# SSM stage with real and imaginary parts stacked on 128 partitions, in a two-block kernel on one core

## The chip, the cores and the metric

One NeuronCore of a Trainium2 chip runs the whole program, one launch for each call. The metric is the device time of that core in microseconds (us), from the kernel's runs on the chip. Engines are named as in the profile: PE is the matrix engine, PEld its weight loads, DVE, ACT and POOL are VectorE, ScalarE and GpSimd, and SP is the queue engine that starts most of the weight transfers.

## What is computed

The program runs two transformer-like blocks on 512 tokens (and 16 meta tokens in front) with a model width of 1024. The first block mixes a chunked gated linear attention (GLA, four heads) with a grouped diagonal state space layer (SSM), and then has a feed-forward part. The second block has latent attention, a causal convolution and a mixture of 32 experts. Only the SSM of the first block is touched here. Cut to what matters, the reference is:

```python
# 64 groups of 16 channels, 64 complex states for each group
lam = exp(dt * (a_re + 1j * a_im))                 # per group and state
bb  = (lam - 1) / (a_re + 1j * a_im) * (b_re + 1j * b_im)
x_t = lam * x_{t-1} + bb @ u_t                     # 64 states, complex
y_t = Re(c @ x_t) + d_skip * u_t
g_s = gelu(y)                                      # on to a gated linear unit
```

## The kernel before

Matrix products of the large weights are made from an upper and a lower part of each operand (three products, `mm3`, lines 93 to 100), in a stream of 128x128 weight loads with up to 512 columns. `Weights` (line 503) loads a block of 1 MB on SP's queue, ACT makes the upper part (line 74) and DVE the lower one (line 75), one block ahead of its use. Both rings have two buffers.

The SSM works on chunks of eight tokens. There are 64 groups; groups q and q + 32 make a pair, and eight *eighths* of four pairs go through the same steps:

- `sincos_exp` (line 144) makes the powers lambda^0..8 (`pw`) and the scaled B (`bb`), with the states of the two groups of a pair on partitions 0 to 63 and 64 to 127 and the real and the imaginary part in the free dimension. Lines 269 to 273 lay `bb` out as a block-diagonal operand `bd`, cleared by POOL and copied by ACT.
- `ssm_states` (line 277) makes the state that each chunk contributes, `ssm_scan` (line 323) carries it through the chunks on POOL: 64 dependent steps of three small operations each.
- `ssm_prep` (line 334) makes C times the powers, `CL`, by six operations on 128x576 elements (lines 350 to 356). They run on DVE; for the first two eighths (`EARLY`) five of the six run on POOL. Eight products of `CL` with `bd` (line 362), real part and then imaginary part summed, give a *strip* of taps, 32 rows (two groups of 16) by 128 for each pair. ACT copies the strip (line 366), DVE adds the skip weights (line 367), and POOL's queue stores it into `k_dram` (line 368).
- `ssm_load` (line 372) reads u from DRAM on POOL's queue, and from `k_dram` eight shifted copies of the strips as the Toeplitz matrices `Tb`, half of them on SP's queue and half on POOL's (line 379).
- `ssm_main` (line 384) has ACT copy the carried states into a block-diagonal operand `HB` (line 390). For each pair it makes two products of 64 weight columns with `Tb` (line 396), one in each column half of the array, and then two of 128 weight columns with `HB` against `CL` (line 400), real and imaginary. ACT applies the gelu and stores the rows.

All of these operands are full fp32: each such product is two instructions on PE, here called *passes*. `ssm_out` (line 411) strings prep, load and main together with two yields in each eighth, and `block` weaves it between steps of the large products: the projections and chains of the GLA heads, then `z_gla` and `mix_gla`, one step being 24 products of 512 columns in the last two. `HB` is one tile, cleared once by POOL on lines 2110 to 2112, behind the scan in POOL's program. The order of each engine's instructions is set when the program is built, by a scheduler that takes what is ready in the order of the text; `issue_after` pins a few places. Every engine then runs its list in order.

The lines that the steps below touch most:

```python
  M = nc.gpsimd if ei < EARLY else V
  ...
  nc.tensor.matmul(p[:32, q * 128:(q + 1) * 128], lhsT=e.bd[:, ri, q0 + q]..., rhs=CL[:, ri, q, 0:8]..., start=(ri == 0), stop=(ri == 1))
  ...
  nc.tensor.matmul(y[64 * g2:64 * g2 + 64, ...], lhsT=U[:, g2, q, 2:66], rhs=T[:, q, g2, :], ...)
  nc.tensor.matmul(o, lhsT=HB[:, q, ri, :], rhs=CL[:, ri, q, 1:9]..., ...)
```

Of the kernel before, what the change touches and what calls it, by code (L numbers as in the profile page):

```python
# [57 lines left out]
def helpers(e):  # L58
# [62 lines left out]
    def rsqrt_act(pool, sumsq, inv_n, n, p=128):  # L121
        """1 / sqrt from ScalarE's square root and one step of Newton's."""
# [21 lines left out]
def sincos_exp(e, sp, mid, keep):  # L144
    """lambda = exp(dt (a_re + i a_im)), bbar, and the powers lambda^0..8, on [128 (g2, n), 32 q]."""
# [123 lines left out]
    bd = keep.tile([128, 2, 32, 2, 16], F32, name="bd", bufs=1)  # L269
    nc.gpsimd.memset(bd, 0.0)  # L270
    for g2 in range(2):
        P = slice(64 * g2, 64 * g2 + 64)
        nc.scalar.copy(bd[P, :, :, g2], bb[P])
    e.pw, e.lam, e.bb, e.bd = pw, lam, bb, bd


def ssm_states(e, sp):
    """Chunk-end states: sum_j lambda^(7-j) bbar u_j, into e.H[:, c, ri, q]; an eighth of the pairs at a step."""
# [55 lines left out]
def ssm_prep(e, sp, ei):  # L334
    """The Toeplitz matrices (taps inside a chunk) and the carry-in matrices of the pairs of eighth ei."""
    nc, A = e.nc, e.A
    V = nc.vector
    q0 = 4 * ei
    cr = sp.tile([128, 2, 4, 16], F32, name="craw", bufs=2)
    nc.gpsimd.dma_start(cr, A["ssm_c"][:, :, q0:q0 + 4, :])  # L340
    dsk = sp.tile([32, 4, 16], F32, name="dsk", bufs=2)
    nc.gpsimd.dma_start(dsk, A["d_diag"][:, q0:q0 + 4, :])
    CL = sp.tile([128, 2, 4, 9, 16], F32, name="CL", bufs=2)
    t = sp.tile([128, 4, 9, 16], F32, name="CLt", bufs=1)
    pr = e.pw[:, 0, :, q0:q0 + 4].rearrange("p k q -> p q k")[:, :, :, None].to_broadcast([128, 4, 9, 16])
    pi = e.pw[:, 1, :, q0:q0 + 4].rearrange("p k q -> p q k")[:, :, :, None].to_broadcast([128, 4, 9, 16])
    c_r = cr[:, 0][:, :, None, :].to_broadcast([128, 4, 9, 16])
    c_i = cr[:, 1][:, :, None, :].to_broadcast([128, 4, 9, 16])
    M = nc.gpsimd if ei < EARLY else V
    M.tensor_mul(CL[:, 0], pr, c_r)  # L350
    M.tensor_mul(t, pi, c_i)
    M.tensor_sub(CL[:, 0], CL[:, 0], t)
    t2 = sp.tile([128, 4, 9, 16], F32, name="CLt", bufs=1)
    M.tensor_mul(CL[:, 1], pr, c_i)
    M.tensor_mul(t2, pi, c_r)
    V.scalar_tensor_tensor(CL[:, 1].rearrange("p q k h -> p (q k h)"),
                           CL[:, 1].rearrange("p q k h -> p (q k h)"), -1.0,
                           t2.rearrange("p q k h -> p (q k h)"), op0=OP.mult, op1=OP.subtract)
    p = e.ps()
    for q in range(4):  # L360
        for ri in range(2):
            nc.tensor.matmul(p[:32, q * 128:(q + 1) * 128],
                             lhsT=e.bd[:, ri, q0 + q].rearrange("p g h -> p (g h)"),
                             rhs=CL[:, ri, q, 0:8].rearrange("p k h -> p (k h)"), start=(ri == 0), stop=(ri == 1))
    stt = sp.tile([32, 4, 128], F32, name="strip", bufs=1)
    nc.scalar.copy(stt, p[:32].rearrange("p (q n) -> p q n", q=4))
    V.tensor_add(stt[:, :, 0:16], stt[:, :, 0:16], dsk)
    nc.gpsimd.dma_start(e.k_dram[q0:q0 + 4, :, 112:240].rearrange("q g n -> g q n"), stt)
    return CL

# [52 lines left out]
def row_rms(e, pool, parts, n, d_inv, rsqrt=None):  # L423
    """1 / sqrt(mean of squares + eps) of n rows given in parts along the free axis."""
# [10 lines left out]
def normed(e, pool, x, g_row, sh_row=None, rsqrt=None):  # L435
    """rmsnorm of 128 token rows x by g_row (plus sh_row)."""
# [10 lines left out]
def turn(e, xs, hi, lo, t):  # L447
    """Token tile t transposed and split into hi, lo[:, k, t * 128..]."""
# [15 lines left out]
def proj_f(e, w, m, xn, spans):  # L464
    """Columns m*128.. of the weight block w as features on partitions; one PSUM tile for each span of tokens."""
# [2063 lines left out]
```

## Time and profile before

| what | value |
|---|---|
| runs | 1563.92, 1561.77, 1563.57 us; median 1563.57 |
| span of the profiled execution | 1561.5 us (its own time is not listed apart from the three runs, which lie 0.3 to 2.4 us above the span) |
| PE busy | 1477.2 us, 95% of the span |
| DVE, ACT, POOL busy | 889.9, 647.6, 541.4 us |
| mean granted clock of PE | 0.977 |
| PE busy from 276.3 to 428.0 us | 151.68 of 151.70 us |

The span runs from the first instruction to the last. Busy time is the union of an engine's instructions; matmuls overlap in it, so a row's duration is longer than the step from one matmul to the next, and steps are read from start times.

### The profile page before, as it was taken

The page shows a single profiled execution, that of the slowest core. Times are in us where ns is not written, and L with a number is a line of the kernel's source. Part 1 is how long each engine was busy: PE and PEld are TensorE (multiplying, and loading weights), DVE is VectorE, ACT ScalarE, POOL GpSimd, SP SyncE. Part 2 cuts the span into 40 slices and gives each one's busy share as a digit, 9 for nine tenths or more (in the row PEclk, how much of TensorE's full clock was granted, in tenths as well). Part 3 has the DMA queues.
Part 4 walks back from the last instruction along what each step waited for, and adds up shares of the span by engine and source line. Part 5 has one row for each costly group of instructions (what it writes and reads, how often), then busy time and mean ns, then how long its engine had stood idle before and what let it go on. Part 6 is the DMA issues. An engine that isn't in the chain of part 4 may idle for free. (4 is left out here: it accounts for less than half of the span.)

```text
span 1561.5 us, 23775 instructions
## 1 busy us (share of the span) xinstructions
PE 1477.2 (95%) x9408; PEld 1249.8 (80%) x9408; DVE 889.9 (57%) x1546; ACT 647.6 (41%) x1055; POOL 541.4 (35%) x605
## 2 busy tenths in 40 slices
PE   7999998999999999999999999899998999988994
PEld 7989997777788889898897888898777877975552
DVE  6585554546324465753645354755689786544554
ACT  6454333334223244323313123447776773342333
POOL 0456888222100030321303012416778723112104
PEclk9999998999999999999999999899999999997998
DMA  6841221548433351664554355321222235877997
GB/s 216 185 104 57 82 89 62 134 145 249 107 128 122 108 200 44 202 195 154 192 176 155 115 163 183 107 76 64 85 78 71 92 132 204 324 290 263 414 412 181
DMA packets 71386, 248.17 MB, mean 159 GB/s; under 512 B 20656, under 2 KB 25536, under 8 KB 54628
## 3 DMA queue, kind: packets, MB, share of 16 engines
q1 hardware_dynamic: 37104, 178.09, 31.8%
q0 software_dynamic: 15936, 48.42, 11.5%
q10 hardware_dynamic: 18228, 20.07, 4.3%
q8 instruction: 76, 1.25, 0.3%
q14 instruction: 42, 0.34, 0.1%
HBM read 223.97 MB, written 29.55 MB: 162 GB/s over the span
## 5 line engine op out<-in xcount | busy, mean ns | idle before, releaser
L75 DVE TENSOR_TENSOR wlo<-raw,whi 128x2048 fp32r<-128x2048 f32 x73 | 179.2, 2455 | 118.7 <-ACT whi L74 118.3
L74 ACT CAST whi<-raw 128x2048 fp32r<-128x2048 f32 x76 | 144.9, 1907 | 193.5 <-PE ps L99 103.3
L1131 POOL TENSOR_TENSOR uc<-uc,u 128x512 f32<-128x512 f32 x77 | 113.8, 1478 | 76.4 <-ACT u L1128 70.0
L99 PE MATMUL ps<-wlo,hh 128*128 128x256 f32 x416 | 117.9, 285 | 2.2 <-DVE wlo L75 2.2
L98 PE MATMUL ps<-xhi,whi 128*128 128x264 f32 (+1 forms) x352 | 119.3, 340 | 0.0
L99 PE MATMUL ps<-xlo,whi 128*128 128x264 f32 (+1 forms) x352 | 118.2, 336 | 0.3 <-DVE xlo L1944 0.3
L98 PE MATMUL ps<-whi,hh 128*128 128x256 f32 x416 | 117.7, 285 | 0.0
L100 PE MATMUL ps<-xhi,wlo 128*128 128x264 f32 (+1 forms) x352 | 117.6, 334 | 0.0
L100 PE MATMUL ps<-whi,hl 128*128 128x256 f32 x416 | 117.3, 283 | 0.0
L100 PE MATMUL ps<-hn,wlo 128*128 128x512 f32 (+1 forms) x256 | 97.7, 383 | 0.0
L99 PE MATMUL ps<-hn,whi 128*128 128x512 f32 (+1 forms) x256 | 97.7, 382 | 0.0
L98 PE MATMUL ps<-hn,whi 128*128 128x512 f32 (+1 forms) x256 | 97.6, 383 | 0.0
L919 POOL TENSOR_TENSOR fr<-fr 128x512 f32<-128x512 f32 x32 | 53.0, 1655 | 112.7 <-ACT fr L918 112.5
L99 PEld LDWEIGHTS ps<-wlo,hh 128*128 128x128 f32 x416 | 79.9, 192 | 3.4 <-DVE wlo L75 2.4
L98 PEld LDWEIGHTS ps<-whi,hh 128*128 128x128 f32 x416 | 79.7, 192 | 1.9 <-issue 1.7
L880 DVE SCALAR_TENSOR_TENSOR aacc<-araw,ca,aacc 128x1024 f32<-128x1024 f32 x42 | 55.7, 1326 | 43.9 <-DMA araw<-in_ada_w_dram 43.5
L100 PEld LDWEIGHTS ps<-whi,hl 128*128 128x128 f32 x416 | 80.1, 193 | 0.0
L98 PE MATMUL ps<-whi,xhi 128*128 128x256 f32 x256 | 75.6, 295 | 0.8 <-ACT H L558 0.8
L876 POOL DMA_DIRECT2D araw<-in_ada_w_dram x48 | 26.1, 544 | 144.5 <-DVE aacc L880 86.3
L100 PE MATMUL ps<-whi,xlo 128*128 128x256 f32 x256 | 75.0, 293 | 0.0
L99 PE MATMUL ps<-wlo,xhi 128*128 128x256 f32 x256 | 74.2, 290 | 0.0
L100 PEld LDWEIGHTS ps<-xhi,wlo 128*128 128x128 f32 x352 | 66.4, 189 | 7.0 <-issue 0.2
(682 smaller groups left out, 4247.1 us busy)
## 6 DMA issues: line engine op xcount, KB each, us to landing
raw<-in_w_ff_dram SPq DMA_DIRECT2D x32, 1024.0 KB
wg<-in_w_eg_dram SPq DMA_DIRECT2D x26, 1024.0 KB
araw<-in_ada_w_dram POOLq DMA_DIRECT2D x48, 512.0 KB, 4.7
wd<-in_w_ed_dram SPq DMA_DIRECT2D x10, 1024.0 KB
raw<-in_w_glu_dram SPq DMA_DIRECT2D x8, 1024.0 KB
wse<-in_w_eg_dram SPq DMA_DIRECT2D x6, 1024.0 KB
y_dram<-wd SPq DMA_DIRECT2D x9, 512.0 KB
U<-u_dram POOLq DMA_DIRECT2D x16, 264.0 KB, 3.8
```

Of the source, the lines that this page charges most:

```text
L74: nc.scalar.copy(hi[:, :n], raw[:, :n])
L75: sub.tensor_sub(lo[:, :n], raw[:, :n], hi[:, :n])
L98: nc.tensor.matmul(out, lhsT=ah, rhs=bh, start=(first and i == 0), stop=False)
L99: nc.tensor.matmul(out, lhsT=ah, rhs=bl, start=False, stop=False)
L100: nc.tensor.matmul(out, lhsT=al, rhs=bh, start=False, stop=(last and i == n - 1))
L876: nc.gpsimd.dma_start(raw, A["ada_w_2"][k * 128:(k + 1) * 128, i * DM:(i + 1) * DM])
L880: V.scalar_tensor_tensor(acc, raw, e.ca[:, k:k + 1], acc, op0=OP.mult, op1=OP.add)
L919: nc.gpsimd.tensor_mul(r, r, r)
L1131: nc.gpsimd.tensor_add(y, y, tmp)
```

## The change

The real and the imaginary part of a group's states are stacked on the 128 partitions. The scaled B becomes one [128, 65, 16] tile `bs` (real part above imaginary part, one slice of zeros at the end), the powers get a second layout `pws`, and `CL` has one slice for each group with C's signs folded in, from three operations on 128x1152 elements. A strip is one product for each group, over all 128 partitions; its weights are 32 columns, the group's 16 and the next group's 16, whose 16 rows of result are not used. The eight groups of an eighth go to four tiles of 32 columns of the array, two rounds. In `ssm_main` the carried states of a group become a 64-column operand `HS` (four copies of 64x256 by ACT), and each group has one product with it in its own column half. `HB`, its clearing and `bd` are gone. `k_dram` has 32 rows for each of 64 groups, of which 16 are read. Docstrings that were removed are not shown.

```diff
 def sincos_exp(e, sp, mid, keep):
...
-    bd = keep.tile([128, 2, 32, 2, 16], F32, name="bd", bufs=1)
-    nc.gpsimd.memset(bd, 0.0)
+    bs = keep.tile([128, 65, 16], F32, name="bs", bufs=1)
+    nc.gpsimd.memset(bs[:, 64], 0.0)
+    ps = keep.tile([128, 2, 9, 64], F32, name="ps", bufs=1)
     for g2 in range(2):
         P = slice(64 * g2, 64 * g2 + 64)
-        nc.scalar.copy(bd[P, :, :, g2], bb[P])
-    e.pw, e.lam, e.bb, e.bd = pw, lam, bb, bd
+        for ri in range(2):
+            nc.scalar.copy(bs[64 * ri:64 * ri + 64, g2:64:2], bb[P, ri])
+        nc.scalar.copy(ps[0:64, :, :, g2::2], pw[P])
+        nc.scalar.activation(ps[64:128, 0, :, g2::2], pw[P, 0], AF.Copy, scale=-1.0)
+        nc.scalar.copy(ps[64:128, 1, :, g2::2], pw[P, 1])
+    e.pw, e.lam, e.bb, e.bs, e.pws = pw, lam, bb, bs, ps
...
 def ssm_prep(e, sp, ei):
...
-    M.tensor_mul(CL[:, 0], pr, c_r)
-    M.tensor_mul(t, pi, c_i)
-    M.tensor_sub(CL[:, 0], CL[:, 0], t)
-    t2 = sp.tile([128, 4, 9, 16], F32, name="CLt", bufs=1)
-    M.tensor_mul(CL[:, 1], pr, c_i)
-    M.tensor_mul(t2, pi, c_r)
-    V.scalar_tensor_tensor(CL[:, 1].rearrange("p q k h -> p (q k h)"),
-                           CL[:, 1].rearrange("p q k h -> p (q k h)"), -1.0,
-                           t2.rearrange("p q k h -> p (q k h)"), op0=OP.mult, op1=OP.subtract)
+    M.tensor_mul(CL, power(0), coeff(0))
+    M.tensor_mul(t, power(1), coeff(1))
+    M.tensor_sub(CL, CL, t)
     p = e.ps()
-    for q in range(4):
-        for ri in range(2):
-            nc.tensor.matmul(p[:32, q * 128:(q + 1) * 128],
-                             lhsT=e.bd[:, ri, q0 + q].rearrange("p g h -> p (g h)"),
-                             rhs=CL[:, ri, q, 0:8].rearrange("p k h -> p (k h)"), start=(ri == 0), stop=(ri == 1))
-    stt = sp.tile([32, 4, 128], F32, name="strip", bufs=1)
-    nc.scalar.copy(stt, p[:32].rearrange("p (q n) -> p q n", q=4))
+    for s in range(2):
+        for j in range(4):
+            g = 4 * s + j
+            nc.tensor.matmul(p[32 * j:32 * j + 32, s * 128:(s + 1) * 128],
+                             lhsT=e.bs[:, g0 + g:g0 + g + 2].rearrange("p g h -> p (g h)"),
+                             rhs=CL[:, g, 0:8].rearrange("p k h -> p (k h)"), start=True, stop=True)
+    stt = sp.tile([128, 2, 128], F32, name="strip", bufs=1)
+    nc.scalar.copy(stt.rearrange("p s n -> p (s n)"), p[:, :256])
     V.tensor_add(stt[:, :, 0:16], stt[:, :, 0:16], dsk)
-    nc.gpsimd.dma_start(e.k_dram[q0:q0 + 4, :, 112:240].rearrange("q g n -> g q n"), stt)
+    nc.gpsimd.dma_start(e.k_dram[g0:g0 + 8, :, 112:240].rearrange("(s j) h n -> (j h) s n", j=4), stt)
     return CL
...
 def ssm_load(e, sp, ei):
...
-    T = sp.tile([128, 4, 2, 128], F32, name="Tb", bufs=1)
-    kd = e.k_dram[q0:q0 + 4]
+    T = sp.tile([128, 8, 128], F32, name="Tb", bufs=1)
+    kd = e.k_dram[8 * ei:8 * ei + 8, 0:16]
...
 def ssm_main(e, sp, ei, CL, U, T):
     nc = e.nc
     q0 = 4 * ei
-    HB = e.HB[ei % len(e.HB)]
+    HS = sp.tile([128, 4, 2, 64], F32, name="HS", bufs=1)
     for g2 in range(2):
-        P = slice(64 * g2, 64 * g2 + 64)
-        nc.scalar.copy(HB[P, :, :, 64 * g2:64 * g2 + 64],
-                       e.H[P, 1:65, :, q0:q0 + 4].rearrange("p c r q -> p q r c"))
+        for ri in range(2):
+            nc.scalar.copy(HS[64 * ri:64 * ri + 64, :, g2],
+                           e.H[64 * g2:64 * g2 + 64, 1:65, ri, q0:q0 + 4].rearrange("p c q -> p q c"))
     y = e.ps()
     for q in range(4):
-        o = y[:, q * 128:(q + 1) * 128]
+        o = [y[64 * g2:64 * g2 + 64, q * 128:(q + 1) * 128] for g2 in range(2)]
         for g2 in range(2):
-            nc.tensor.matmul(y[64 * g2:64 * g2 + 64, q * 128:(q + 1) * 128],
-                             lhsT=U[:, g2, q, 2:66], rhs=T[:, q, g2, :], start=True, stop=False,
+            nc.tensor.matmul(o[g2], lhsT=U[:, g2, q, 2:66], rhs=T[:, 2 * q + g2], start=True, stop=False,
                              skip_group_check=True)
-        for ri in range(2):
-            nc.tensor.matmul(o, lhsT=HB[:, q, ri, :], rhs=CL[:, ri, q, 1:9].rearrange("p k h -> p (k h)"),
-                             start=False, stop=(ri == 1), skip_group_check=True)
+        for g2 in range(2):
+            nc.tensor.matmul(o[g2], lhsT=HS[:, q, g2], rhs=CL[:, 2 * q + g2, 1:9].rearrange("p k h -> p (k h)"),
+                             start=False, stop=True, skip_group_check=True)
...
-    e.HB = [sp.tile([128, 4, 2, 128], F32, name=f"HB{i}") for i in range(1)]
-    for t in e.HB:
-        nc.gpsimd.memset(t, 0.0)
```

## Rows read from the trace of the kernel before

**Rows 1.** The page's head and its busy times with the share of the span.

```profile
span 1561.5 us, 23775 instructions
PE 1477.2 (95%) x9408; PEld 1249.8 (80%) x9408; DVE 889.9 (57%) x1546; ACT 647.6 (41%) x1055; POOL 541.4 (35%) x605
```

**Rows 2.** Stretches: length, busy us of PE, PEld, DVE, ACT, POOL; PEclk, DMA share, GB/s.

```profile
254.00:261.30 7.30, 0.11 (x1) 0.00 (x0) 1.16 (x1) 5.25 (x11) 7.13 (x11) 0.77 0.28 93
261.30:268.20 6.90, 6.86 (x26) 6.03 (x27) 6.90 (x3) 3.43 (x5) 6.53 (x7) 0.50 0.00 0
268.20:276.30 8.10, 6.64 (x49) 5.88 (x48) 7.93 (x9) 0.60 (x1) 6.71 (x4) 1.00 0.43 138
276.30:428.00 151.70, 151.68 (x862) 116.62 (x863) 72.96 (x142) 57.53 (x76) 33.32 (x59) 1.00 0.56 157
```

**Rows 3.** PE's timeline over one steady eighth: start, length, line, tiles, count.

```profile
373.11 0.39 PE L100 MATMUL ps<-ohi,wlo 128*128 128x512 f32 x1
373.43 0.44 PE L396 MATMUL ps<-Tb,U 128*64 128x128 f32 x4
373.80 0.71 PE L400 MATMUL ps<-CL,HB 128*128 128x128 f32 x4
...
377.62 0.39 PE L99 MATMUL ps<-olo,whi 128*128 128x512 f32 x1
...
382.63 0.39 PE L100 MATMUL ps<-ohi,wlo 128*128 128x512 f32 x1
382.95 0.41 PE L362 MATMUL ps<-CL,bd 128*32 128x128 f32 x2
...
386.01 1.72 PE L362 MATMUL ps<-CL,bd 128*32 128x128 f32 x14
...
387.99 0.39 PE L98 MATMUL ps<-ohi,whi 128*128 128x512 f32 x1
...
390.84 0.44 PE L396 MATMUL ps<-Tb,U 128*64 128x128 f32 x4
```

**Rows 4.** Passes of the strips and of the Tb products: duration ns min/median/max, starts, shapes.

```profile
L362 PE MATMUL ps<-CL,bd x128: 272/273/297, 273.1 to 404.9; 128*32 128x128 f32 x128
L396 PE MATMUL ps<-Tb,U x128: 272/298/324, 295.3 to 426.4; 128*64 128x128 f32 x128
```

**Rows 5.** ACT's timeline behind the scan; in brackets the idle time before and its releaser.

```profile
255.88 2.12 ACT L390 COPY HB<-H 64x512 f32<-64x512 f32 x2 [13.03 <-POOL HB L2112]
...
261.05 0.24 ACT L667 COPY kT<-ps 32x128 f32<-32x128 f32 x1
```

**Rows 6.** Who waited for whom from 240 to 277 us: total us, times, longest.

```profile
PE ps L676 <- ACT kT L667: 7.2, 1, 7.2
...
PE ps L679 <- DVE St L680: 1.5, 1, 1.5
```

**Rows 7.** POOL's timeline in the same stretch.

```profile
254.90 0.95 POOL L2112 MEMSET HB<- 128x1024 f32 x1
...
259.04 1.23 POOL L350 TENSOR_TENSOR CL<-pw,craw 128x576 f32<-128x576 f32 x1
...
264.92 1.41 POOL L352 TENSOR_TENSOR CL<-CL,CLt 128x576 f32<-128x576 f32 x1
```

**Rows 8.** DVE's timeline in the same stretch.

```profile
260.14 6.47 DVE L637 TENSOR_TENSOR E<-E,k 128x256 f32<-128x256 f32 x1 [11.00 <-ACT E L635]
...
269.11 0.76 DVE L356 SCALAR_TENSOR_TENSOR CL<-CL,CLt 128x576 f32<-128x576 f32 x1
...
275.27 1.00 DVE L680 SCALAR_TENSOR_TENSOR St<-St,dc,ps 128x256 f32<-128x256 f32 x2
```

**Rows 9.** Waits of ACT's weight casts from 276 to 440 us: total us, times, longest.

```profile
ACT whi L74 <- PE ps L99: 18.4, 8, 4.6
```

**Rows 10.** The loads of Tb from k_dram (line 379): us from issue to landing.

```profile
DMA to landing us min/median/max: 3.4/4.4/5.7
```

**Rows 11.** The copies of the block-diagonal B on ACT: duration ns, first and last start.

```profile
L273 ACT COPY bd<-bb x2: 1047/1066/1084, 50.4 to 51.5; 64x1024 f32<-64x1024 f32 x2
```

More of the change, by code (lines that the diff above doesn't have):

```diff
@@ L337, in ssm_prep @@
     V = nc.vector
[L338 to L345, printed above, removed]
@@ L346, in ssm_prep @@
-    pi = e.pw[:, 1, :, q0:q0 + 4].rearrange("p k q -> p q k")[:, :, :, None].to_broadcast([128, 4, 9, 16])
-    c_r = cr[:, 0][:, :, None, :].to_broadcast([128, 4, 9, 16])
-    c_i = cr[:, 1][:, :, None, :].to_broadcast([128, 4, 9, 16])
-    M = nc.gpsimd if ei < EARLY else V
-    M.tensor_mul(CL[:, 0], pr, c_r)
-    M.tensor_mul(t, pi, c_i)
-    M.tensor_sub(CL[:, 0], CL[:, 0], t)
-    t2 = sp.tile([128, 4, 9, 16], F32, name="CLt", bufs=1)
-    M.tensor_mul(CL[:, 1], pr, c_i)
-    M.tensor_mul(t2, pi, c_r)
@@ L365, in ssm_prep @@
-    stt = sp.tile([32, 4, 128], F32, name="strip", bufs=1)
-    nc.scalar.copy(stt, p[:32].rearrange("p (q n) -> p q n", q=4))
+    g0 = 8 * ei
+    cr = sp.tile([128, 2, 8, 16], F32, name="craw", bufs=2)
+    nc.gpsimd.dma_start(cr, A["ssm_c"][:, :, g0:g0 + 8, :])
+    dsk = sp.tile([128, 2, 16], F32, name="dsk", bufs=2)
+    nc.gpsimd.dma_start(dsk, A["d_diag"][:, ei])
+    CL = sp.tile([128, 8, 9, 16], F32, name="CL", bufs=2)
+    t = sp.tile([128, 8, 9, 16], F32, name="CLt", bufs=1)
+    power = lambda i: e.pws[:, i, :, g0:g0 + 8].rearrange("p k g -> p g k")[:, :, :, None].to_broadcast([128, 8, 9, 16])
@@ new lines, in ssm_prep @@
+    coeff = lambda i: cr[:, i][:, :, None, :].to_broadcast([128, 8, 9, 16])
+    M = nc.gpsimd if ei < EARLY else V
+    M.tensor_mul(CL, power(0), coeff(0))
+    M.tensor_mul(t, power(1), coeff(1))
+    M.tensor_sub(CL, CL, t)
+    p = e.ps()
+    for s in range(2):
[4 more added lines that the diff above has]
+                             rhs=CL[:, g, 0:8].rearrange("p k h -> p (k h)"), start=True, stop=True)
@@ L373, in ssm_load @@
     nc = e.nc
-    q0 = 4 * ei
-    U = load_u(e, sp, q0, 1)
-    T = sp.tile([128, 4, 2, 128], F32, name="Tb", bufs=1)
-    kd = e.k_dram[q0:q0 + 4]
+    U = load_u(e, sp, 4 * ei, 1)
+    T = sp.tile([128, 8, 128], F32, name="Tb", bufs=1)
+    kd = e.k_dram[8 * ei:8 * ei + 8, 0:16]
     for k in range(8):
         (nc.gpsimd if k % 2 else nc.sync).dma_start(T[16 * k:16 * k + 16],
-                            kd[:, :, 16 * k:16 * k + 128].rearrange("q (g h) n -> h q g n", g=2))
+                                                    kd[:, :, 16 * k:16 * k + 128].rearrange("g h n -> h g n"))
     return U, T
@@ L1971, in block @@
     e.u2_dram = dram("u2_dram", [128, 2, 32, NCH])
-    e.k_dram = dram("k_dram", [32, 32, 240])
+    e.k_dram = dram("k_dram", [64, 32, 240])
     e.gs_dram = dram("gs_dram", [SEQ, DM])
@@ L2064, in block @@
             nc.gpsimd.memset(kz, 0.0)
-            nc.gpsimd.dma_start(e.k_dram.rearrange("q (a r) n -> (q a) r n", r=8)[:, :, 0:112], kz[:, None, :].to_broadcast([128, 8, 112]))
+            nc.gpsimd.dma_start(e.k_dram[:, 0:16, 0:112], kz[0:64, None, :].to_broadcast([64, 16, 112]))
         gates(e, gtp, wa, wgu, bp)
@@ L2498, in prepare @@
     A["ssm_b"] = np.stack([gnh(g["b_re"][0]), gnh(g["b_im"][0])], 1)
-    ghn = lambda a: a.reshape(2, 32, 16, 64).transpose(0, 3, 1, 2).reshape(128, 32, 16)
-    A["ssm_c"] = np.stack([ghn(g["c_re"][0]), ghn(g["c_im"][0])], 1)
-    dd = np.zeros((2, 16, 32, 16), np.float32)
-    d = g["d_skip"][0].reshape(2, 32, 16)
+    ngh = lambda a: a.reshape(2, 32, 16, 64).transpose(3, 1, 0, 2).reshape(64, 64, 16)
+    cre, cim = ngh(g["c_re"][0]), ngh(g["c_im"][0])
+    A["ssm_c"] = np.stack([np.concatenate([cre, cim]), np.concatenate([cim, cre])], 1)
+    dd = np.zeros((4, 32, 8, 2, 16), np.float32)
+    d = g["d_skip"][0].reshape(2, 32, 16).transpose(1, 0, 2).reshape(8, 2, 4, 16)
     for h in range(16):
-        dd[:, h, :, h] = d[:, :, h]
-    A["d_diag"] = dd.reshape(32, 32, 16)
+        dd[:, h, :, :, h] = d[:, :, :, h].transpose(2, 0, 1)
+    A["d_diag"] = dd.reshape(128, 8, 2, 16)
     return {k: np.ascontiguousarray(v) for k, v in A.items()}
```

## The prediction

> **What bounds the kernel now.** I read the page first: PE is busy for 95% of the span and no other engine comes near [rows 1]. An average over many stages settles nothing for one of them, so the second view is busy time by stretch [rows 2]. The reader should see two different regimes there. From 276.3 to 428.0 us, where seven of the eight strips and all eight `ssm_main` parts lie, PE is busy for 151.68 of 151.70 us at the full clock level (2.4 GHz), while DVE, ACT and POOL are busy for half of the time or less: PE is the limit, and PE time that goes away should come off the end. From 254.0 to 276.3 us it is the other way round: PE hardly works for 7.3 us, then runs for 6.9 us at a granted clock of 0.50 (1.2 GHz), then has another gap.
>
> The third view is PE's timeline of one steady eighth [rows 3]. It repeats every 390.84 - 373.43 = 17.41 us. Inside it lie two steps of 24 large products. Their step is (382.63 - 377.62) / 22 = 0.228 us, so 48 take 10.93 us. `ssm_main` takes what lies between its two neighbours less two such steps: 377.62 - 373.11 - 0.46 = 4.05 us. The strips take the rest, 17.41 - 10.93 - 4.05 = 2.43 us. Eight eighths of 6.5 us are some 52 us of PE, in which only small fp32 products run. One pass of 128 columns costs (1.72 - 0.273) / 13 = 0.111 us behind another one [rows 3, 4]. Going into a narrow tile costs 373.43 - 373.11 - 0.23 = 0.09 us more than a step, and coming out 387.99 - 386.01 - 14 x 0.111 - 0.23 = 0.20 us, so 0.29 us for each visit [rows 3]. Now look at a Tb row: four passes of 0.272 us or more end 0.44 us after the first began [rows 3, 4]. In one line they would need 0.27 + 3 x 0.111 = 0.60 us. So the two column halves work at the same time already, but the visit ends after one pass on top of the other, and HB products over the full width follow.
>
> The fourth view is who waits in the bad stretch. ACT stands 13.03 us before the first HB copy, whose releaser is the clearing of `HB` [rows 5], and PE's 7.2 us wait is for a copy (kT) that stands behind it on ACT [rows 6]. The clearing begins at 254.90, when POOL is through with the scan [rows 7]. PE's second wait, 1.5 us, is for DVE's L680 at 275.27 [rows 6, 8]. DVE is late because an operation on 256 elements took 6.47 us [rows 8] while POOL ran its share of the prep from 259.04 on [rows 7].
>
> Nothing else holds the PE-bound part: all eight weight casts there that waited did so for PE to free a buffer, none for a transfer [rows 9].
>
> **The change part by part.**
>
> *Main products.* Per eighth, eight visits' worth of switching between half tiles and full width go away. 32 passes remain, all in half tiles, 16 for each half, and the halves overlap as the Tb row shows: 16 x 0.111 + 0.29 = 2.07 us in place of 4.05, so 1.98 us less, 15.8 us in all. The bound on the bad side is the same 32 passes with no more overlap than a full line, 3.84 us (1.7 us saved in all); I take the overlap, since the row for this very tile shape shows it.
>
> *Strips.* 16 passes remain, in four tiles of 32 columns. Four at once is in no row. Bounds: no overlap, 16 x 0.111 + 0.29 = 2.07 us; all four at once, 4 x 0.111 + 0.29 = 0.73 us. I take 0.73, because the nearest row, the halves, overlaps fully. Pairs only would give 1.18. A single `CL` also means that a strip is one visit, where two passes went ahead of the other fourteen [rows 3]. Saved per eighth: 2.43 - 0.73 = 1.70 us; seven in the PE-bound part give 11.9 us. The first strip lies in front of PE's second wait and counts below.
>
> The Trainium skill ("TensorE: Matmul & The Clock Gate", Part 3, packing small matmuls) measured a speedup of 2.38 for three column tiles. Kept at that ratio, four would give an estimated 3.2, strips of 0.85 us and a sum worse by 0.8 us. No row here shows four tiles.
>
> *The first stretch.* Without the clearing, the copies can start 0.95 us sooner [rows 7]. Four copies of half the size replace two: between 2.12 us (same elements) and 4.24 us (each as long as one now) [rows 5]; I take 2.5, nearer to the elements. PE resumes 0.6 us earlier (bounds 0.95 earlier, 1.2 later) and does its first strip faster. Both only bring it sooner to the wait for L680, so they earn nothing there. When does L680 come? POOL's part becomes six operations of 1152 elements, 2.1 to 2.46 us each (twice 1.23 at most), 14.8 us at most; a POOL operation seems to shut out DVE until a pause. DVE loses the two 0.76 us operations of line 356, one of them ahead of L680 [rows 8]. Best: everything keeps its place and L680 comes 0.95 + 0.76 earlier, at 273.6. Worst: all POOL work goes first, from 258.1 to 272.9, and then what DVE does now from 269.11 to 275.27, so 279.1. I take the middle, 276.4, 1.1 us later than now. PE then idles for some 4.5 us. An idle time of 7.3 us was followed by 6.9 us at the lower clock, which costs 3.45 us, and one of 1.5 us by none [rows 2, 6]; with 4.5 midway I put 1.7. This stretch loses 2.8 us (bounds: 1.7 gained, 7.3 lost).
>
> The Trainium skill ("SBUF — State Buffer", SBUF: two separate sides) says that the port pair of DVE and GpSimd is an exclusive lock, held for the whole instruction. The 6.47 us row agrees, and by it the worst case would be the likely one, with a time 4.4 us above my forecast.
>
> *What I cost at nothing.* DVE's prep: six operations of 0.76 us become three on the same elements, beside 10.9 us of large products. ACT's copies: at most 2.1 us more for an eighth, and ACT is free for 94 of 151.7 us [rows 2]. If that cover went, main would start later by those 2.1 us. The strip store has twice the rows; `Tb` loads stay as they are and land after 4.4 us, 5.7 at most [rows 10]. On POOL's queue they are issued behind u, and the next store stands behind them, as now. The next main comes 11.7 us after the last in place of 13.4, which leaves some 4 us. In `sincos_exp` ACT gets about 3.6 us more (ten copies in place of two of 1.07 us) near 50 us [rows 11], against PSUM evacuation with eight banks of slack, and POOL loses one clearing.
>
> *Sum.* 15.8 + 11.9 - 2.8 = 24.9 us. The page's span, 1561.5 us, lies 2.1 us under the median of the runs, 1563.57, and the same amount comes off both: 1563.6 - 24.9 = **1538.7 us**.
>
> **The rivals.**
>
> *Column tiles overlap less than the halves suggest.* For it: no row has four. Against it: the Tb row. Pairs only cost 7 x 0.45 = 3.2 us more, 1541.9; none, 7 x 1.34 = 9.4 us more, 1548.1.
>
> *The HS copies go to an earlier place on ACT, and it ends slower.* The place is ACT's list: HB's copies already stand ahead of what PE needs, and the scheduler may place copies that no longer wait for a clearing still further ahead. Each microsecond that ACT blocks earlier is one more of PE idle. Now ACT blocks from 242.85 on. It turns slower than before when that moves ahead by more than the 24.9 us saved, to about 218; at 30 us ahead it gives 1569. Against it: only 0.95 us of the wait is the clearing's. The mirror image, copies behind kT, would save 7.2 us of idle and 3.45 of clock: 1528.
>
> *The Toeplitz chain takes over.* Main waits for store, loads and main again. If landing took twice the 4.4 us, the slack of 4 us would be gone and the eighth would lose the rest of it and more: with the period going back to 17 us, 7 x 3.3 us are lost, 1562. Against it: longest landing 5.7 us.
>
> *The new order scatters the small products.* Each group that is put alone among large ones costs a visit of 0.29 us: 64 groups of main, 18.6 us, so 1557. For it: the strips were split in two. Against it: in the steady eighths main stays together.
>
> **How the numbers follow.** Forecast 0.58; less overlap 0.16; slower order on ACT 0.07; the mirror image 0.05; Toeplitz chain 0.07; scattered order 0.07. The predicted time is that of the first. The range goes down to 1529 (the mirror image, about) and up to 1553: no strip overlap (1548.1) with the worst first stretch of 4.5 us more. What lies outside is the two cases at 1557 and above and the slower one, about 0.2. A measurement of this kernel can tell 0.2%, 3.1 us, from no change. Faster by more than that: forecast, overlap, mirror, scattered and part of the chain, 0.88; within, the rest of the chain and part of the slower order, 0.06; slower, 0.06.
>
> **What would show it.** In the changed profile: `ssm_main` near 2.1 us between its neighbours and 16 strip passes within 0.7 us; a period near 13.8 us; PE still busy throughout that part; casts still waiting for PE; PE's wait behind kT still there, near 6.5 us, and the one for L680 longer. Wrong would be: passes of different tiles in one line, PE idle before Tb products, or HS copies that start ahead of the scan's end and block ACT for much more than 12 us.

## The result, and the profile after

The changed kernel took 1547.51 us (median of four runs, 1546.0 to 1549.16), the kernel before 1563.74 in the four runs beside it (1561.77 to 1566.02). The ratio is 0.9896, with an interval from 0.9882 to 0.991: 16 us faster, where 24.9 were forecast. The profiled execution took 1547.29 us with a span of 1545.2, 16.3 us under that of before.

The page's head and busy times of the changed kernel, as [rows 1]:

```profile
span 1545.2 us, 23773 instructions
PE 1452.4 (94%) x9408; PEld 1234.7 (80%) x9408; DVE 887.0 (57%) x1526; ACT 651.3 (42%) x1079; POOL 541.4 (35%) x600
```

PE works 24.8 us less (1477.2 less 1452.4), but the span gives back only 16.3 of them: PE stands idle for 8.5 us more than before. (That 24.8 is so near the forecast is chance: the forecast has 2.8 us of added waiting in it, which is no busy time.) The stretches show where. The columns are as in [rows 2]:

```profile
254.00:261.00 7.00, 0.32 (x1) 0.32 (x2) 3.76 (x1) 6.81 (x15) 6.98 (x6) 0.66 0.36 118
261.00:268.00 7.00, 2.84 (x7) 1.59 (x7) 6.99 (x3) 3.07 (x4) 6.98 (x4) 0.50 0.06 19
268.00:277.00 9.00, 9.00 (x54) 8.84 (x53) 8.90 (x9) 0.60 (x1) 4.87 (x3) 0.71 0.42 137
277.00:350.00 73.00, 71.99 (x508) 56.09 (x507) 36.35 (x65) 31.27 (x56) 18.86 (x32) 1.00 0.57 160
350.00:372.00 22.00, 16.52 (x92) 13.20 (x94) 13.79 (x26) 10.20 (x13) 5.34 (x9) 0.85 0.97 314
372.00:415.00 43.00, 43.00 (x288) 34.45 (x285) 20.25 (x36) 16.15 (x21) 9.98 (x17) 1.00 0.60 162
```

Two stretches are bad. The first, up to 277, was bad before too. The other, 350 to 372, is new: in [rows 2] PE was busy without a gap there. The DMA share is 0.97 in it, but the same burst of loads stood in the trace of before (0.97 from 355 to 377 us).

Outside these the change does what it says. PE's timeline over one steady eighth, as [rows 3]:

```profile
384.48 0.44 PE L394 MATMUL ps<-Tb,U 128*64 128x128 f32 x4
384.75 0.39 PE L397 MATMUL ps<-CL,HS 128*64 128x128 f32 x4
...
386.38 0.50 PE L98 MATMUL ps<-ohi,whi 128*128 128x512 f32 x1
...
391.72 0.39 PE L100 MATMUL ps<-ohi,wlo 128*128 128x512 f32 x1
392.04 0.64 PE L361 MATMUL ps<-CL,bs 128*32 128x128 f32 x16
392.61 0.50 PE L98 MATMUL ps<-ohi,whi 128*128 128x512 f32 x1
...
398.32 0.44 PE L394 MATMUL ps<-Tb,U 128*64 128x128 f32 x4
```

`ssm_main` takes 386.38 - 384.48 = 1.90 us from its first product to the next large one, the 16 strip passes 0.57 likewise, the period is 398.32 - 384.48 = 13.84 us. All three were named beforehand (2.1, under 0.7, 13.8).

Who made PE wait, from 240 to 430 us (total us, times, longest), as [rows 6] for the first stretch:

```profile
PE ps L673 <- ACT kT L664: 6.9, 1, 6.9
PE ps L99 <- DVE wlo L75: 4.2, 1, 4.2
PE ps L394 <- DMA Tb<-k_dram: 3.3, 1, 3.3
PE ps L361 <- DVE CL L356: 2.2, 1, 2.2
PE ps L698 <- DVE St L693: 0.9, 1, 0.9
```

**The first stretch.** ACT, DVE and POOL there, as [rows 5], [rows 7] and [rows 8]:

```profile
252.74 2.54 ACT L388 COPY HS<-H 64x256 f32<-64x256 f32 x4 [13.46 <-POOL H L337]
255.31 1.90 ACT L74 CAST whi<-raw 128x2048 fp32r<-128x2048 f32 x1
...
260.39 0.24 ACT L664 COPY kT<-ps 32x128 f32<-32x128 f32 x1
```

```profile
257.24 10.12 DVE L75 TENSOR_TENSOR wlo<-raw,whi 128x2048 fp32r<-128x2048 f32 x1 [21.51 <-ACT whi L74]
```

```profile
255.97 2.26 POOL L354 TENSOR_TENSOR CL<-ps,craw 128x1152 f32<-128x1152 f32 x1
...
262.61 2.60 POOL L356 TENSOR_TENSOR CL<-CL,CLt 128x1152 f32<-128x1152 f32 x1
```

The HS copies moved two places ahead on ACT: they now stand in front of a weight cast and the small copy `vm` too. So the lower half `wlo` (line 75) comes after the scan, just when POOL's prep runs, and takes 10.12 us in place of the 2.29 us that it takes elsewhere. PE's second wait is now for `wlo`, not for `St`.

**The middle stretch.** PE's timeline from 355 to 373 us:

```profile
355.33 0.39 PE L100 MATMUL ps<-xhi,wlo 128*128 128x512 f32 x1
357.88 0.64 PE L361 MATMUL ps<-CL,bs 128*32 128x128 f32 x16 [2.16 <-DVE CL L356]
358.46 0.68 PE L98 MATMUL ps<-ohi,whi 128*128 128x512 f32 x1
...
361.92 0.45 PE L100 MATMUL ps<-ohi,wlo 128*128 128x512 f32 x1
...
365.42 0.39 PE L100 MATMUL ps<-ohi,wlo 128*128 128x512 f32 x1
369.13 0.69 PE L394 MATMUL ps<-Tb,U 128*64 128x128 f32 x4 [3.32 <-DMA Tb<-k_dram]
...
372.54 0.50 PE L98 MATMUL ps<-ohi,whi 128*128 128x512 f32 x1
```

Elsewhere the step from a large product to a visit is 392.04 - 391.72 = 0.32 us. So the wait for CL costs 357.88 - 355.33 - 0.32 = 2.23 us and that for Tb 369.13 - 365.42 - 0.32 = 3.39. Behind each of them PE runs at about half speed: eight large products take 361.92 - 358.46 = 3.46 us where the same eight behind the strips at 392.61 take 1.98, and this `ssm_main` takes 372.54 - 369.13 = 3.41 where others take 1.90. Together 2.23 + 3.39 + 1.48 + 1.51 = 8.6 us.

Why are they late? ACT, DVE and POOL ahead of that main (one fence each):

```profile
344.00 0.69 ACT L701 ACTIVATE ot<-ps,hg 128x512 f32<-128x512 f32 x1 [4.34 <-DMA o_dram<-ot]
...
346.87 0.37 ACT L365 COPY strip<-ps 128x256 f32<-128x256 f32 x1
...
351.75 1.05 ACT L736 CAST ohi<-o 128x1024 fp32r<-128x1024 f32 x1 [4.51 <-DMA o<-o_dram]
```

```profile
352.84 1.23 DVE L737 TENSOR_TENSOR olo<-o,ohi 128x1024 fp32r<-128x1024 f32 x1 [3.92 <-ACT ohi L736]
353.98 1.35 DVE L354 TENSOR_TENSOR CL<-ps,craw 128x1152 f32<-128x1152 f32 x1
```

```profile
355.63 0.70 POOL L346 DMA_DIRECT2D craw<-in_ssm_c_dram  x1 [4.43 <-DVE CL L354]
356.41 2.13 POOL L377 DMA_DIRECT2D Tb<-k_dram  x4
```

The strip of the fifth eighth left PE at about 342, but its copy stands on ACT behind an `ot` that waits 4.34 us for the transfer of the `ot` before it (one buffer). Then POOL can't issue that eighth's Tb loads, since `craw` is in front of them in its queue and waits for DVE's line 354, which stands behind `olo`, which waits for `ohi` and the loads of `o`. These four loads themselves land later than the 5.7 us of [rows 10], by 365.9 us:

```profile
DMA to landing us min/median/max: 2.9/4.1/8.0
```

Later still are the other four, on SP's queue (in the trace of before they were issued from 363.8 to 366.4 us, ahead of a main at 373.4). SP waits 5.0 us for a load of `w_o` and 4.1 us for loads of the gate first, and issues the last at about 365; PE gets `Tb` at 369.1:

```profile
359.97 5.51 SPq L377 DMA_DIRECT2D Tb<-k_dram  x4
```

**Position by position.** The runs were made on several chips, and the program reaches this part up to 7.5 us earlier or later on one than on another. So the next table counts from one event of each run's own trace: the start of ACT's last copy of `v` before the bad stretch (238.1 us before, 237.7 after). "Main 1" is the first Tb product of the first eighth, "1 to 4" the time from there to main 4, "end" the last Tb product of all, "rest" what lies from there to the span's end. All in us, worked out from start times in the trace and rounded so that each row adds up. The runs of the next section are already in it.

| run | main 1 | 1 to 4 | 4 to 6 | 6 to end | end | rest |
|---|---|---|---|---|---|---|
| before | 57.3 | 60.6 | 34.9 | 35.5 | 188.3 | 1135.1 |
| after | 59.1 | 51.2 | 36.5 | 28.3 | 175.1 | 1132.4 |
| hs_late | 58.8 | 51.2 | 37.8 | 28.3 | 176.1 | 1133.4 |
| before_late | 60.4 | 60.6 | 34.9 | 35.6 | 191.5 | 1133.9 |
| ot_two | 67.3 | 51.2 | 33.1 | 28.3 | 179.9 | 1133.4 |
| olo_late | 59.3 | 51.2 | 38.5 | 28.3 | 177.3 | 1132.8 |
| hs_kt3 | 59.7 | 51.1 | 36.3 | 28.3 | 175.4 | 1136.4 |
| before_kt3 | 59.0 | 60.7 | 34.9 | 35.5 | 190.1 | 1130.6 |
| ot_in_st | 59.0 | 51.1 | 32.7 | 28.3 | 171.1 | 1134.1 |
| tb_pool | 59.0 | 51.2 | 35.4 | 28.3 | 173.9 | 1131.3 |
| mid_three | 59.0 | 51.1 | 41.4 | 28.3 | 179.8 | 1135.0 |
| prep_dve | 53.7 | 51.1 | 37.5 | 28.3 | 170.6 | 1133.8 |
| prep_dve_hs | 53.9 | 51.1 | 37.5 | 28.3 | 170.8 | 1136.2 |
| all_moved | 50.8 | 51.2 | 33.7 | 28.3 | 164.0 | 1131.8 |

The second and the fourth column repeat to 0.1 us in every kernel with the new operands. The third doesn't: of the runs that leave that stretch alone, it lies between 36.3 and 37.8. The rest varies by 5.8 us, although no edit lies in it. Main 1 lies between 58.8 and 59.3 in the runs of the changed kernel that leave the first stretch alone; but before_late, whose order is that of the kernel before, comes 3.1 us later there than before does. PE's second wait is 2.6 us in it in place of 1.5, and the granted clock behind it 0.55 and then 0.63 (up to 285 us), where before has 1.00 from 277 us on.

### The profile page after: what moved, and what is told of

Read it like the earlier page. It is cut to its first block, busy times and chain, and to the rows that moved or that the text cites. A ratio compares the mean times of both kernels' runs of the same rounds, so it can differ in the third digit from the quotient of the medians.

```text
span 1545.2 us, 23773 instructions
## 1 busy us (share of the span) xinstructions
PE 1452.4 (94%) x9408; PEld 1234.7 (80%) x9408; DVE 887.0 (57%) x1526; ACT 651.3 (42%) x1079; POOL 541.4 (35%) x600
## 5 line engine op out<-in xcount | busy, mean ns | idle before, releaser
L75 DVE TENSOR_TENSOR wlo<-raw,whi 128x2048 fp32r<-128x2048 f32 x73 | 185.8, 2546 | 138.7 <-ACT whi L74 138.7
L98 PEld LDWEIGHTS ps<-xhi,whi 128*128 128x128 f32 x352 | 66.0, 188 | 7.9 <-issue 1.5
```

What stands on the lines that cost most here:

```text
L75: sub.tensor_sub(lo[:, :n], raw[:, :n], hi[:, :n])
L98: nc.tensor.matmul(out, lhsT=ah, rhs=bh, start=(first and i == 0), stop=False)
```

## The experiments

Ratios are to the kernel before on the same chip, which took 1564.8 us (median) in the first set of runs, 1570.65 in the second, 1568.73 in the third and 1564.61 in the last. The changed kernel's own is 0.9896. In the edits, `behind(e, (x,))` puts the instructions under it behind x in their engine's list; `e.kts`, `e.cl` and `e.sc` hold kT copies by head, and last prep operations and strip copies by eighth.

**First set: single waits.** Theory: the loss of the middle stretch and that of the first each have one releaser.

```diff
# hs_late: the HS copies of the first eighth behind the second head's kT
+            with behind(e, (e.kts[1],) if ei == 0 else ()):
                 nc.scalar.copy(HS[64 * ri:64 * ri + 64, :, g2], ...)
```

> The changed kernel, with the four HS copies of the first eighth put behind the kT copy of the second head on ACT; nothing else. Theory (ACT's list): the copies stand ahead of a weight cast and of kT and block ACT until the scan is through, so PE's wait for kT (6.9 us) and for the lower weight part (4.2 us) and the half clock behind them go, and the time falls by 9 us, between 5 and 13, to about 1538.5. Rival (the lock between POOL and DVE, and the scan itself, set the pace whatever the order): PE waits as long elsewhere, and the time stays within 3 us of 1547.5.

Ratio 0.9906 [0.9887, 0.9925], and the order on ACT is the same as without the edit: the kT that PE waits for is the third head's, and the second head's was long past. So nothing was tested, and the run stands as a repeat of the changed kernel.

```diff
# before_late: in the kernel before, the HB copies behind the same kT
+        with behind(e, (e.kts[1],) if ei == 0 else ()):
             nc.scalar.copy(HB[P, :, :, 64 * g2:64 * g2 + 64], ...)
```

> The kernel before, with the two HB copies of the first eighth put behind the kT copy of the second head on ACT. Theory (ACT's list): PE's wait of 7.2 us for kT and the 3.45 us of half clock go, the second wait for L680 may stay: 7 to 11 us less than before, about 1554.5, which would show that this loss is not of the change's making. Rival (the lock between POOL and DVE): less than 3 us.

Ratio 1.0 [0.9988, 1.0012], for the same reason; a repeat of the kernel before.

```diff
# ot_two: a second buffer for ot, out of a ring that other tiles of the chain use
-        ot = pool.tile([128, 512], F32, name="ot", bufs=1)
+        ot = pool.tile([128, 512], F32, name="ot", tag="d", bufs=2)
```

> The changed kernel, with two buffers for the output tile ot of the heads (in the ring of the tiles d1 and d5). Theory (ACT's list near 340 us): the second ot no longer waits 4.3 us for the first one's transfer, the strip copy behind it and the loads of o come 4 us earlier, and PE's waits near 355 (2.6 us) and 365 us (3.7 us) shrink: 2 to 6 us less, about 1543.5. Rival (the burst of 4 MB of transfers near 350 us sets the pace): the same bytes land at the same rate, the Tb loads are as late, and the time changes by less than 2 us.

Ratio 0.9947 [0.9926, 0.9968]. The wait for Tb fell to 1.9 us and "4 to 6" to 33.1, but the shared ring made a new wait in the first stretch (PE's waits, 240 to 430 us), and main 1 comes 8.2 us later:

```profile
PE ps L648 <- DVE E L628: 20.4, 1, 20.4
```

```diff
# olo_late: the four olo subtractions behind the prep of the sixth eighth on DVE
-        V.tensor_sub(olo[:, 2 * h:2 * h + 2], r, ...)
     yield
+    with behind(e, (e.cl[5],)):
+        for h in range(4):
+            V.tensor_sub(olo[:, 2 * h:2 * h + 2], o[:, 2 * h:2 * h + 2], ...)
```

> The changed kernel, with the four subtractions that make the lower part of o put behind the prep of the sixth eighth on DVE. Theory: PE's wait of 2.6 us for CL near 355 us goes, with the 1.8 us of half clock behind it; the wait for Tb near 365 us grows by a part of that, since the transfers are no earlier. 1 to 4 us less, about 1545. Rival (transfers alone): PE only waits longer for Tb, and the time changes by less than 1 us.

Ratio 0.9913 [0.9893, 0.9932]: no gain. The wait for CL is gone, and the one for Tb took all of it:

```profile
PE ps L394 <- DMA Tb<-k_dram: 7.5, 1, 7.5
```

So Tb ends last in the middle stretch, and CL is only what is next.

**Second set: the right kT, and the start of the Tb chain.**

```diff
# hs_kt3 (and before_kt3 with HB in the kernel before): behind the third head's kT
+            with behind(e, (e.kts[2],) if ei == 0 else ()):
```

> The changed kernel with the four HS copies of the first eighth put behind the kT copy of the third head on ACT (in the earlier run they were put behind the second head's kT, which had long been done, so nothing moved). Theory (ACT's list: the blocked copies hold up the weight cast, kT and with them PE): PE's 6.9 us wait for kT and its 4.2 us wait for wlo both go, the half clock of some 7 us behind them goes too, and the time falls by 8 to 13 us, to 1535 to 1540 us. Rival 1 (POOL's share of the prep holds DVE up, whatever ACT does): the kT wait goes, but a wait for DVE of 4 us or more stays or grows; gain 2 to 5 us, 1543 to 1546. Rival 2 (what is won early is given back between 350 and 372 us, where transfers set the pace): the waits go, but those for CL and Tb grow by as much; 1546 to 1550.

Ratio 0.9905 [0.9881, 0.9928], main 1 at 59.7 in place of 59.1: no gain, with the kT wait gone. Its place was taken by others (PE's waits, the three of the first stretch), because `wlo` still took 10 us beside POOL's prep (DVE's timeline):

```profile
PE ps L677 <- DVE St L678: 7.0, 1, 7.0
PE ps L361 <- POOL CL L356: 3.6, 1, 3.6
...
PE ps L677 <- ACT St L675: 1.8, 1, 1.8
```

```profile
266.37 10.04 DVE L75 TENSOR_TENSOR wlo<-raw,whi 128x2048 fp32r<-128x2048 f32 x1 [8.98 <-ACT whi L74]
```

Rival 1 is right about the wait, though not about its 2 to 5 us of gain: POOL's share of the prep ends last, and taking ACT's list away alone gives nothing.

In the kernel before, the same edit on HB:

> The kernel before with its two HB copies of the first eighth put behind the same kT copy. If the early loss was there before the change (theory: it stands in ACT's list, and the change only made it a little longer): the 7.2 us wait and the half clock behind it go, 8 to 11 us less, 1553 to 1556 us. If it is mostly of the change's making: at most 4 us less, 1560 or more. Beside the run above this also says whether the changed kernel's advantage grows or shrinks when both are rid of it.

Ratio 0.9993 [0.9981, 1.0005]. The kernel before has the same second limit: its 7.2 us wait for kT [rows 6] went, and 4.9 us for DVE's `St`, 2.2 for ACT's and 2.0 for POOL's CL came. Main 1 comes at 59.0, between the two traces without the edit.

```diff
# ot_in_st: the last ot of all into St, which nobody reads any more
+        if h == 3 and dv:
+            ot = St[:, 0:2].rearrange("p b d -> p (b d)")
+        else:
             ot = pool.tile([128, 512], F32, name="ot", bufs=1)
```

> The changed kernel, where the last ot tile (fourth head, second half) is written into St, which nobody reads any more, so that ACT need not wait 4.3 us for the transfer of the ot before it. Theory (the Tb chain of the fifth eighth is late because the strip copy stands behind that ot on ACT): strip copy near 343 in place of 346.9, Tb lands 3 to 4 us earlier, PE's wait for Tb goes from 3.3 to under 1 us; 2 to 4 us less, 1543.5 to 1545.5. Rival (the transfers between 350 and 365 us, some 16 engines full, set the pace): Tb lands no more than 1 us earlier, 1546.5 to 1549.

Ratio 0.9876 [0.9854, 0.9897], which overlaps the changed kernel's; but "4 to 6" is at 32.7, 3.6 us under the lowest of its repeats. The strip copy came 3.2 us earlier, counted from the same event, and of PE's waits Tb's fell to 1.9 us:

```profile
PE ps L361 <- DVE CL L356: 2.8, 1, 2.8
PE ps L394 <- DMA Tb<-k_dram: 1.9, 1, 1.9
```

The place of that copy on ACT is thus a cause of the loss. The same bytes moved in this run, so the full DMA engines alone don't explain it. They may still have a part: Tb still ends last, and SP issues the last of its four only at 369.7 us, after 6.6 us of waits for loads of the gate.

```diff
# tb_pool: all Tb loads of the fifth eighth from POOL
-        (nc.gpsimd if k % 2 else nc.sync).dma_start(...)
+        (nc.gpsimd if k % 2 or ei == 4 else nc.sync).dma_start(...)
```

> The changed kernel, where all eight Tb loads of the fifth eighth are issued by POOL; before, four of them stood on SP behind waits for the w_o and gate loads (5.0 and 4.1 us). Theory (SP's queue is what makes the last Tb land late): the wait for Tb goes from 3.3 us to under 1, 2 to 4 us less, 1543.5 to 1545.5. Rival (the transfers' own time, or the strip copy at its start): the wait stays at 2.5 us or more, 1546.5 to 1549.

Ratio 0.9913 [0.9894, 0.9932], the Tb wait at 4.3 us: no gain that can be told from the spread. POOL's queue was itself held up by `craw`, as above, and had all eight loads to issue, so that SP's queue is not the limit alone.

**Third set: the edits together, and POOL's prep.** In mid_three the diffs of ot_in_st, olo_late and tb_pool stand in one kernel.

> The changed kernel with three edits that only touch the stretch around 350 us: the last ot in St (strip copy no longer behind the transfer of the ot before), the olo subtractions behind the sixth eighth's CL on DVE, and all Tb loads of the fifth eighth on POOL. Theory (three waits in a row stand one behind another: take one away and the next ends last, so each alone gives little): with all three away the waits for CL and Tb are under 1.5 us together in place of 5.5, no half clock behind them, and the time is 5 to 9 us less than the changed kernel's, a ratio to before of 0.984 to 0.9865. Rival (the transfers of the stretch, all 16 engines full for 15 us, set the pace): waits of 4 us or more remain, for Tb or for ohi and olo, a ratio of 0.987 to 0.990.

Ratio 0.9956 [0.994, 0.9973], worse than without them. Main 5 came 17.1 us after main 4, though 3.1 us of the Tb wait stayed; ot_in_st alone has 18.8, the repeats of the changed kernel 20.8 to 22.5, and a steady period is 13.8. But then PE waited 7.4 us for the CL of the seventh eighth: the three edits changed the order behind them, and DVE stood in front of that prep until the positions for the rotary tables had landed:

```profile
PE ps L361 <- DVE CL L356: 7.4, 1, 7.4
```

```profile
376.21 0.20 DVE L1052 CAST rtx<-pi 128x64 f32<-128x64 int32 x1 [8.59 <-DMA pi<-in_pos_dram]
```

So up to main 5 the three together gave more than the best of them alone, as the theory has it, but not its 1.5 us of waits; for the whole time the verdict is open from this run, which shows another such wait.

```diff
# prep_dve
-EARLY = 2
+EARLY = 0
```

> The changed kernel with EARLY = 0: the prep of the first two eighths on DVE too, none on POOL; HS stays where it is on ACT. Theory (POOL's prep shuts DVE out, so that wlo took 10.1 us, and PE waited 4.2 us for it, at half clock before and behind): wlo takes 2.3 us again, that wait is under 1 us, PE's wait for kT stays near 6.9; 3 to 6 us less, a ratio of 0.986 to 0.988. Rival (DVE's own prep, 1.36 us an operation, stands in wlo's place): the wait for DVE stays at 3 us or more, a ratio of 0.989 or above.

Ratio 0.9863 [0.9846, 0.9879], main 1 at 53.7, 5.4 us earlier. DVE's `wlo` takes 2.28 us again, and PE waits for kT alone up to 290 us, with ACT's list as it was:

```profile
263.04 2.28 DVE L75 TENSOR_TENSOR wlo<-raw,whi 128x2048 fp32r<-128x2048 f32 x1
```

Then with the diff of hs_kt3 on top, as prep_dve_hs:

> EARLY = 0 and the HS copies of the first eighth behind the third head's kT, together. Alone the second took the kT wait away and got waits of 7.0 us for DVE's St, 3.6 for POOL's CL and 1.8 for ACT's St in its place. Theory (the early stretch has two limits, ACT's list and POOL's prep, and either hides the other): with both away PE waits for less than 4 us in all between 250 and 285 us, in place of 11 to 12.4, with little half clock; 8 to 12 us less than the changed kernel, a ratio of 0.982 to 0.9845. Rival (PE waits for the end of the scan on POOL whatever the order, since HS, CL and the weights' low halves all follow it): 7 us or more of waits remain; a ratio of 0.987 or above.

Ratio 0.9881 [0.9863, 0.9899], main 1 at 53.9: no better than `EARLY = 0` alone. PE waits for `wlo` (first line below) and 1.4 us more for `St`, 6.7 us in all. Now DVE itself stands in front of everything, at the first prep operation, whose `craw` POOL issues behind the scan:

```profile
PE ps L99 <- DVE wlo L75: 5.3, 1, 5.3
```

```profile
262.61 1.36 DVE L354 TENSOR_TENSOR CL<-ps,craw 128x1152 f32<-128x1152 f32 x1 [19.76 <-DMA craw<-in_ssm_c_dram]
```

The rival of this run comes out, with 6.7 us for its 7: in this order too, a list has an operation that needs the end of the scan in front of what PE needs.

**The last run** takes that away on both lists, adds the middle edits, and moves the load of the positions:

```diff
# all_moved: mid_three and EARLY = 0, and
+    with behind(e, (e.last_sub,) if ei == 0 else ()):      # first prep behind the second wlo
         M.tensor_mul(CL, power(0), coeff(0))
...
+            with behind(e, (e.sc[0],) if ei == 0 else ()):  # HS behind the first strip copy
                 nc.scalar.copy(HS[64 * ri:64 * ri + 64, :, g2], ...)
...
+    with behind(e, (e.sc[7],)):                             # positions behind the last strip copy
         nc.scalar.dma_start(pi, A["pos8"])
```

> The changed kernel with the early and the middle stretch cleared together. Early: the prep of the first two eighths on DVE, the first of it behind the second wlo, and the first eighth's HS copies behind its strip copy on ACT, so that nothing PE needs stands behind the end of the scan. Middle: the three edits of the run before last in that stretch (ot in St, olo behind CL, Tb of the fifth eighth on POOL), with the load of the rope positions behind the last strip copy, since in that run DVE stood behind this load and CL came 7.4 us late. Theory (two stretches of PE idle, each with several releasers one behind another, are what the predicted 24.9 us lack): waits under 4 us and no half clock between 250 and 285 us, under 4 us in the middle stretch, and 15 to 22 us less than the changed kernel, a ratio of 0.975 to 0.980. Rival 1 (the scan's end on POOL sets the early stretch, since the first prep needs craw, which POOL issues behind the scan): 5 us or more of waits remain there, for CL or for St behind it; a ratio of 0.981 to 0.984. Rival 2 (transfers set the middle stretch): the early part is won and the Tb wait grows by as much, to over 8 us; a ratio of 0.984 to 0.988.

1536.59 us, ratio 0.9829 [0.9816, 0.9843]: 28 us faster than the kernel before, and about 10.5 us (0.67% of 1564.6) faster than the changed one. All of PE's waits from 240 to 430 us:

```profile
PE ps L362 <- DVE CL L357: 4.9, 1, 4.9
PE ps L396 <- DMA Tb<-k_dram: 3.1, 1, 3.1
PE ps L700 <- DVE St L695: 1.8, 1, 1.8
```

Main 1 comes at 50.8 (8.3 us earlier than after the change), "4 to 6" takes 33.7, no better than in ot_in_st (32.7). The ratio is that of rival 1, and so are the waits: those for kT and `wlo` are gone, and 4.9 us for CL and 1.8 for `St` behind it remain. The reason is a little different. DVE waits only 0.4 us for the first eighth's `craw`; but the last operation of the first prep (line 357) stands on DVE behind the first operation of the second, which waits for the second eighth's `craw`, also issued behind the scan. That wait is 2.35 of the 4.9 us:

```profile
264.14 1.36 DVE L355 TENSOR_TENSOR CL<-ps,craw 128x1152 f32<-128x1152 f32 x1 [2.35 <-DMA craw<-in_ssm_c_dram]
...
266.87 1.35 DVE L357 TENSOR_TENSOR CL<-CL,CLt 128x1152 f32<-128x1152 f32 x1
```

In the middle stretch the Tb wait is still 3.1 us, with a granted clock of 0.84 from 350 to 372. The eight loads, all on POOL's queue now, take 6.5 to 7.9 us to land (median 7.4), where [rows 10] has 4.4. With 4.4 the last, issued at 350.8 us, would by this estimate have landed 2.2 us sooner.

## Why the prediction was right in part, and where it was short

**Main products and strips: right.** Measured as the prediction did it (from the large product in front, at 384.16 us, to the second one behind, at 386.71, less two steps), `ssm_main` went from 4.05 us to 2.09 (2.07 forecast). The strips, again the rest of the period, went from 2.43 to 13.84 - 10.93 - 2.09 = 0.82 (0.73 forecast). The period fell by 3.57 us where 3.68 were due. Four column tiles overlap as fully as two: the rival of less overlap, the likeliest one, is out, and with it the ratio of 2.38 that I had from the Trainium skill ("TensorE: Matmul & The Clock Gate", Part 3). "6 to end" shows it without a wait: 35.5 - 28.3 = 7.2 us less, where 1.70 for one strip and 3 x 1.98 for three mains make 7.6. "1 to 4" fell by 9.4 where 3 x (1.98 + 1.70) = 11.0 were due; three periods as measured would give 10.7. PE is busy for 51.1 of these 51.2 us, so what is missing is no wait; products of the heads stand among the small ones there, and the cause stays open.

**First stretch: the size about right, the place not.** The prediction lost 2.8 us there and had one strip (1.70) to gain, so main 1 should have come at 57.3 + 2.8 - 1.7 = 58.4; it came at 59.1, behind a new wait of 0.9 us for `St` (line 693) at 293.5 us. With before_late's 60.4 in place of 57.3 it would be 61.5, so the size holds to some 3 us only. But the loss was put on the prep that delays `St`. In this trace it lies in `wlo`, with HS in front of its cast on ACT; with HS further back, in hs_kt3, the next `wlo` took 10 us. That move on ACT was a rival here, and it did happen, by two places only: ACT blocks from 252.74 - 13.46 = 239.3 on, 3.2 us ahead of before (counted from the common event) and far from the 24.9 from which the sign would have turned. That POOL's prep shuts out DVE was the right mechanism: line 75 begins at 257.24 among POOL's operations and ends at 267.37, 2.2 us after the fourth of them, about as long as it takes by itself. The Trainium skill ("SBUF — State Buffer", SBUF: two separate sides) calls this an exclusive lock, and the trace agrees: 2.28 us with the prep off POOL. Here it took a pause of POOL, behind four operations in a row, before DVE came in.

**The mirror image was priced wrongly.** I gave the copies behind kT 7.2 us of idle and 3.45 of clock. With exactly that edit main 1 came at 59.7 in place of 58.8 to 59.3 (hs_kt3), and in the kernel before at 59.0 (before_kt3), between 57.3 and 60.4: nothing was won in either. A wait that ends last at 7 us is worth 7 us only if nothing else ends soon behind it. The busy rows of POOL and DVE in that stretch had shown that something would.

**What I cost at nothing: this step failed.** "`Tb` loads ... land after 4.4 us, 5.7 at most ... which leaves some 4 us." The slack came from a steady eighth. In the fifth, the strip copy waits behind `ot`, POOL's issue behind `craw`, SP's behind loads of `w_o` and the gate, and the landing takes up to 8.0 us. In the kernel before, main 5 came 135.4 us after the common event and did not wait, but POOL's four loads had landed only 2.2 us ahead of it; now PE would have been ready some 11 us sooner, and Tb had landed only by 131.4, 4.0 sooner. The Toeplitz chain was a rival, but as one for all eighths at once; it took over in one, with the sign that the prediction had named for being wrong: PE idle before Tb products. The term of 0 should have been 9.0 ("4 to 6" grew by 1.6 where 2 x 3.68 = 7.4 less was due), 8.6 of which PE's rows name. That ot_in_st wins 3.6 us of it back by moving one copy is shown; ot_two wins 3.2 by another edit of the same wait. The other links of the chain (craw behind olo, SP's queue, the loads themselves) are seen in the trace, but no edit of one of them alone gained anything that stands out of the spread, so their shares are not shown.

**The sum.** 24.9 forecast, less 0.7 (first stretch), 1.6 (1 to 4), 9.0 (4 to 6) and 0.4 (6 to end) is 13.2, which is 188.3 - 175.1. The start of this part gave 0.4 and the rest 2.7 more, which makes 16.3. The 2.7 lie within what the rest varies by from run to run, so I claim nothing for them; without them the gain would have been 13.6. All this is against one trace of before. Against before_late the gain up to "end" is 191.5 - 175.1 = 16.4, and the 3.2 us more lie in the first stretch; the terms from main 1 on don't change. The measured 1547.5 us lies inside the range of 1529 to 1553 by luck: its upper end was drawn for strips without overlap and a worse first stretch, and neither came.

What stays open: how much of the Tb wait in all_moved would go with the loads spread out, and whether the last 4.9 us go when the first prep stands ahead of the second on DVE, or when both `craw` are loaded from a queue that doesn't stand behind the scan. None was tried.

## What to carry to other kernels

When an engine that sets the pace gets faster, look for slack in every period of the loop, not in the steady one: what was hidden in the worst period with little room to spare (here 2.2 us) is the first to show, and here it took a third of the gain that was forecast. In lists that are executed in order, a wait is worth only its distance to the next one behind it, so price it by removing both; and ask of each list whether something that nobody needs soon (HS, `craw`, the positions) stands in front of something that PE needs now. Count positions from an event common to both traces, and compare with repeats: it showed an effect of 3.6 us here that the ratios don't tell from none, and at main 1 two traces of one order lie 3.1 us apart.

## What the runs showed of the hardware

Four 32-column tiles of fp32 products ran fully side by side here, which no row of before could show: the first four of the 16 passes start at 392.039, 392.046, 392.053 and 392.059 us, the next pass in the first tile 0.134 us after the one before it, later ones 0.11.

A short wait can cost half as much again in clock. After the 2.2 us wait at 355 us, eight products ran at steps of 0.43 us, and then at 0.23 again, and after the 3.3 us wait at 365 all of `ssm_main` ran at half speed; the granted clock from 350 to 372 was 0.85. The wait of 1.5 us in the kernel before had no such tail [rows 2, 6], nor had the one of 2.8 us for CL in ot_in_st (granted clock 1.00 from 365.9 to 376 us), so in these runs the length of the wait alone does not tell.
